# A two-layer diffusion transformer on one core: the feed-forward's work written out turn by turn, with every engine taking only what others finished in turns before

## The chip, the cores and the metric

The kernel runs on 1 NeuronCore of one Trainium2 chip. The core has a matrix engine (PE, with weight loads listed apart as PEld), a vector engine (DVE), a scalar engine (ACT), a general engine (POOL) and a queue for transfers (SP). Each works through its own instructions in the order written and waits on semaphores for the others. The metric is the device time of one execution in microseconds (us).

## The reference

Two layers over 512 latent tokens and 256 context tokens of width 1024. Each layer mixes tokens by two kinds of attention, and then runs a SwiGLU feed-forward. Every layer's norms and residuals are modulated by vectors that come from a condition: six rows of 1024 per layer, once for the latents and once for the context.

```python
mod = silu_c @ w_mod[l] + b_mod[l]
mod_c = silu_cc @ w_mod[l] + b_mod[l]
sh1, sc1, g1, sh2, sc2, g2 = jnp.split(mod[:, None, :], 6, axis=-1)
...
x = x + g1 * branch_merge(ya, yb, ga, gb, w_pa[l], w_pb[l], w_o[l])
...
h2 = modulate(rms_norm(x, norm2[l]), sh2, sc2)
x = x + g2 * swiglu(h2, w_ffn_in[l], w_ffn_out[l])      # a, u = split(h @ w_in); (silu(a) * u) @ w_out
if not last:
    hc2 = modulate(rms_norm(ctx, norm2[l]), csh2, csc2)
    ctx = ctx + cg2 * swiglu(hc2, w_ffn_in[l], w_ffn_out[l])
```

The hidden width is 2816, that is 22 blocks of 128 channels. Layer 0 runs the feed-forward on 768 tokens (latents and context), layer 1 on the 512 latents alone.

## The kernel before, in words

All data is float32, and each product is made of three matmuls on halves: an operand is split into an upper part that the matmul keeps exactly and a lower part that holds the rest, and the kernel adds upper·upper, upper·lower and lower·upper. ACT makes an upper part by a copy into the matmul's type, DVE the lower part by a subtraction.

A hidden block `f` needs gate and up weights (two raw tiles `wr` of 128x1024), each in two halves of the contraction, against two halves of the tokens (`nh` is 384 tokens in layer 0, 256 in layer 1). This 2x2 product is made by `quad` with seven products in place of eight, in the way of Strassen and Winograd. The left operands are the quarters A11, A12, A22 and the sums S1 = A21+A22 (in a tile `ws` of its own), S3 = A11-A21, S2 = S1-A11, S4 = A12-S2, written over the raw weights. The right operands are quarters of the activations and their sums, made before. Each product is one **turn** of PE: 12 matmuls (4 blocks of the contraction, 3 halves each). The order of turns, with the last of a block put behind the first of the next, is

A11, A22 of the block before, A12, S1, S2, S4, S3.

Products add up in three PSUM banks, `qu`, `qc` and `qv`. Because a bank is used again by a later turn, ACT first copies it to a tile `tt` (line 1728): `qu` after A11 and after S2, `qv` after S1. The second use of `qv` is turn S4, two turns after S1. Then DVE adds bank and copy (line 2140), ACT takes the silu of the sum (2141), DVE adds and multiplies for the up half (2153, 2154, 2157). The finished block `ph` is split in halves for the second matrix: ACT 1864, DVE 1865. After every four blocks an output part runs over eight column blocks `j`: weights `wfo` are split (ACT 1877, DVE 1881), 12 matmuls of 512 columns into a bank `po` (and in layer 0 another 12 of 256), and DVE adds the gated bank to the residual `x` (1577).

Blocks 0 and 1 (layer 0) and 0 to 2 (layer 1) run in the plain way ahead of this; the other 20 and 19 blocks and four output parts are written by `paced`. It sets the order on PE, DVE and ACT by hand: for each turn it writes first the weight work that later turns need (`load`: the transfer; `hi`: ACT's upper part, line 1585, and in the same call the DVE sums of S1, S2 and S4, lines 2115 to 2123; `lo`: DVE's lower part, line 1589), then the turn's matmuls, then what the bank needs (`take`). Upper parts are written up to three turns ahead and lower parts up to two.

`paced` also works off the modulation vectors: an item is a transfer of 512 KB (`wmodT`) and a DVE multiply-and-sum over 1024 elements for each condition (lines 450 and 452), two for most items of layer 0 and one for the others. An item is written once a count of spare DVE time allows it, both sums at once. The first output part waits (`gated`) until the items of its gate are done. Raw weights, modulation weights and output weights share four buffers `wr`; upper and lower parts share three buffers `wh` and three `wl`. Transfers are issued by SP; their order follows from the order of the code.

Of the kernel before, what the change touches and what calls it, by code (L numbers as in the profile page):

```python
# [331 lines left out]
class Trunk:  # L332
# [112 lines left out]
    def mod_one(self, l, n, crow, junk, w=None):  # L445
        nc, d = self.nc, self.d
        if w is None:
            w = self.raw(d["wmodT"][l * 48 + n])
# [3 lines left out]
        nc.vector.tensor_tensor_reduce(  # L452
            w, w, crow[:, 0], 1.0, 0.0, ALU.mult, ALU.add, self.mod[l][:, 0, n : n + 1])
# [1252 lines left out]
    def quad(self, left, right, kn, nh, take):  # L1706
# [19 lines left out]
        def copy(bank, name):  # L1726
# [15 lines left out]
                 load=left.load if w == "A11" else None, hi=lambda w=w: left.upper(w), lo=lambda w=w: left.lower(w),  # L1742
                 later=take.done if w == "A22" else None)
# [5 lines left out]
    def paced(self, steps, near, beside, ready):  # L1749


        at = [0.0]
        for s in steps:
            at.append(at[-1] + s.cost)
        done = dict(load=0, hi=0, lo=0)
        todo = sum(c for c, *_ in beside)
        share = min(1.0, 1.15 * todo / sum(s.cost - s.busy for s in steps))
        free, wait, late = 0.0, None, deque()
        self.live = 0

        def go(stage, up):
            while done[stage] < up:
                n = done[stage]
                if stage == "hi":
                    go("load", n + 1)
                    go("lo", n - 1)
                elif stage == "lo":
                    go("hi", n + 1)
                done[stage] += 1
                run = getattr(steps[n], stage)  # L1770
                if run:
                    if stage == "load" and self.live + 2 > 4 and wait:
                        beside_now()
                    run()

        def beside_now():
            nonlocal wait, free
            cost, run, w = wait
            run(w)
            self.live -= 1  # L1780
            free -= cost
            wait = None

        def fetch(n):
            nonlocal wait
            cost, load, run = beside.pop(0)
            wait = cost, run, load()
            self.live += 1
            return at[n]

        since = 0.0
        for n, s in enumerate(steps):
            count = lambda ahead: next((i for i in range(n, len(steps)) if at[i] >= at[n] + ahead), len(steps))
            far = count(4 * near + LEAD)
            while done["load"] < far and (not steps[done["load"]].load or self.live <= 2):
                go("load", done["load"] + 1)
            go("lo", max(n + 1, count(3 * near - 0.1)))
            go("hi", max(n + 1, count(4 * near - 0.1)))
            free = min(free + (s.cost - s.busy) * (share if ready() else 1.0), BEHIND)
            while s.gated and not ready():  # L1800
                if not wait:
                    fetch(n)
                beside_now()
            if wait and at[n] - since >= LEAD and free >= 0.7 * wait[0]:
                beside_now()
            if beside and not wait and self.live <= 2:
                since = fetch(n)
# [6 lines left out]
        while late:  # L1814
            late.popleft()()
        while wait or beside:
            if not wait:
                fetch(n)
# [133 lines left out]
    def run(self):  # L1952
# [3 lines left out]
        with (  # L1956
# [23 lines left out]
            for l in range(DEPTH):  # L1980
# [7 lines left out]
                with (  # L1988
# [33 lines left out]
                    def two(of, n, cost, then=None):  # L2022
                        def run(w):
                            self.mod_one(of, n, *rows, w)
                            if then:
                                then()
                        return cost, lambda: self.raw(d["wmodT"][of * 48 + n]), run
# [59 lines left out]
class Step:  # L2087


    def __init__(self, cost, busy, mul, take, load=None, hi=None, lo=None, later=None, gated=False):  # L2090
        self.cost, self.busy, self.mul, self.take = cost, busy, mul, take
        self.load, self.hi, self.lo, self.later, self.gated = load, hi, lo, later, gated


class Quarters:
# [14 lines left out]
    def upper(self, key):  # L2110
# [183 lines left out]
```

## Time and profile before

| | |
|---|---|
| median of 3 runs | 2081.72 us (2074.14 to 2083.82) |
| the profiled execution | 2073.19 us, of which 2070.6 us span |
| PE, PEld busy | 1951.0 us (94%), 1797.1 us (87%) |
| DVE, ACT, POOL busy | 1496.1 us (72%), 942.2 us (46%), 220.3 us (11%) |
| mean granted clock of PE | 0.985 |

The turns written by `paced` run from 654.0 to 1133.1 us (layer 0) and from 1670.2 to 2025.7 us (layer 1). In the views a row `PE qv L1722 <- ACT tt L1728` means that PE's matmuls into bank `qv` at line 1722 had to wait for ACT's copy at line 1728. Windows give the busy time of PE, PEld, DVE, ACT and POOL with the number of instructions, then the granted clock as a share of full speed, then the transfers' share and rate. In the chain of waits each row is a start, a length and a piece of work.

### The profile page before, as it was taken

How to read it: one execution, taken by the hardware profiler on the slowest of the kernel's cores; microseconds unless marked ns; L12 is line 12 of the kernel's file. 1: busy time of each engine (PE TensorE's matmuls, PEld its weight loads, DVE VectorE, ACT ScalarE, POOL GpSimd, SP SyncE). 2: the span in 40 equal slices, each digit the busy share in tenths (PEclk: the TensorE clock that was granted, in tenths of full speed). 3: DMA queues.
4: the chain of work that ended last, by engine and by line, in shares of the span. 5: the costliest groups of instructions: out<-in, count | busy, mean ns of one | idle time of the engine just before them, and what ended most of it. 6: DMA issues, size and time to landing. Idle time of an engine off the chain costs nothing. (4 is left out here: it accounts for less than half of the span.)

```text
span 2070.6 us, 31681 instructions
## 1 busy us (share of the span) xinstructions
PE 1951.0 (94%) x12298; PEld 1797.1 (87%) x12298; DVE 1496.1 (72%) x2813; ACT 942.2 (46%) x1832; POOL 220.3 (11%) x130
## 2 busy tenths in 40 slices
PE   8999999999999898989999999999999989889888
PEld 8989999888999888989888888799888988778777
DVE  7478887797778876776765777887566776666665
ACT  5466666622345323232423546665533453343344
POOL 0422232123000000000000031223100000000000
PEclk9999999999999999999999999999999999999999
DMA  8111112343631332434442421112245313213213
GB/s 308 51 57 47 49 62 70 103 172 133 224 118 41 107 127 83 131 97 148 131 134 74 148 92 37 41 57 75 95 157 211 105 57 97 82 60 104 82 60 121
DMA packets 73110, 214.79 MB, mean 104 GB/s; under 512 B 8704, under 2 KB 10880, under 8 KB 72960
## 3 DMA queue, kind: packets, MB, share of 16 engines
q1 hardware_dynamic: 72960, 212.78, 31.1%
q8 instruction: 96, 1.57, 0.3%
q14 instruction: 54, 0.44, 0.1%
HBM read 200.69 MB, written 6.82 MB: 100 GB/s over the span
## 5 line engine op out<-in xcount | busy, mean ns | idle before, releaser
L1722 PE MATMUL qu<-r,w 128*128 128x384 f32 (+1 forms) x1872 | 304.7, 316 | 8.7 <-ACT tt L1728 5.2
L1722 PEld LDWEIGHTS qu<-r,w 128*128 128x128 f32 x1872 | 288.5, 195 | 17.5 <-ACT tt L1728 7.6
L381 PE MATMUL pj<-h,wh 128*128 128x512 f32 (+1 forms) x704 | 256.8, 365 | 5.6 <-ACT kg L809 1.7
L381 PE MATMUL pj<-h,wl 128*128 128x512 f32 (+1 forms) x704 | 247.2, 351 | 0.0
L381 PE MATMUL pj<-hl,wh 128*128 128x512 f32 (+1 forms) x704 | 246.7, 350 | 0.0
L366 ACT ACTIVATE wh<-wr 128x1024 fp32r<-128x1024 f32 (+2 forms) x157 | 146.0, 936 | 210.0 <-issue 64.0
L1722 PE MATMUL qv<-r,w 128*128 128x384 f32 (+1 forms) x936 | 168.0, 333 | 71.7 <-ACT tt L1728 71.7
L1722 PEld LDWEIGHTS qv<-r,w 128*128 128x128 f32 x936 | 152.5, 207 | 80.9 <-ACT tt L1728 80.8
L1585 ACT ACTIVATE w<-wr 128x512 fp32r<-128x512 f32 x234 | 145.2, 624 | 166.7 <-DVE wr L2119 72.2
L381 PE MATMUL po<-ph,wh 128*128 128x512 f32 (+1 forms) x576 | 197.5, 344 | 1.6 <-ACT ph L1864 0.9
L381 PE MATMUL po<-ph,wl 128*128 128x512 f32 (+1 forms) x576 | 196.1, 342 | 1.5 <-DVE wl L368 1.4
L381 PE MATMUL po<-pl,wh 128*128 128x512 f32 (+1 forms) x576 | 195.8, 340 | 0.0
L1589 DVE TENSOR_TENSOR w<-wr,w 128x512 fp32r<-128x512 f32 x234 | 160.3, 687 | 46.3 <-ACT w L1585 44.1
L368 POOL TENSOR_TENSOR wl<-wr,wh 128x1024 fp32r<-128x1024 f32 (+1 forms) x66 | 145.3, 2205 | 389.9 <-ACT wh L366 383.6
L1577 DVE SCALAR_TENSOR_TENSOR x<-po,G,x 128x256 f32<-128x256 f32 (+3 forms) x168 | 99.3, 596 | 113.5 <-PE po L381 112.0
L381 PEld LDWEIGHTS pj<-h,wh 128*128 128x128 f32 x704 | 133.6, 190 | 20.4 <-ACT kg L809 1.9
L381 PEld LDWEIGHTS pj<-h,wl 128*128 128x128 f32 x704 | 133.2, 189 | 18.1
L381 PEld LDWEIGHTS pj<-hl,wh 128*128 128x128 f32 x704 | 133.8, 190 | 13.7
L505 POOL TENSOR_TENSOR rs<-rs,expo 128x2 f32<-128x2 f32 (+2 forms) x8 | 6.2, 773 | 1224.1 <-DVE rs L504 1224.1
L1009 ACT ACTIVATE pth<-tp 128x512 fp32r<-128x512 f32 x176 | 103.4, 596 | 64.6 <-PE tp L1059 37.1
L1010 DVE TENSOR_TENSOR ptl<-tp,pth 128x512 fp32r<-128x512 f32 x176 | 119.5, 685 | 15.2 <-ACT pth L1009 13.5
L381 PEld LDWEIGHTS po<-ph,wh 128*128 128x128 f32 x576 | 108.4, 188 | 15.9 <-ACT wh L366 2.2
(250 smaller groups left out, 4319.6 us busy)
## 6 DMA issues: line engine op xcount, KB each, us to landing
wr<-wfi SPq DMA_DIRECT2D x88, 512.0 KB, 3.3
wr<-wmodT SPq DMA_DIRECT2D x84, 512.0 KB, 3.3
wr<-win SPq DMA_DIRECT2D x68, 512.0 KB, 3.3
wr<-wfo SPq DMA_DIRECT2D x64, 256.0 KB, 2.7
wr<-wo SPq DMA_DIRECT2D x26, 512.0 KB, 3.6
wr<-wfo SPq DMA_DIRECT2D x26, 384.0 KB, 3.6
wr<-wp SPq DMA_DIRECT2D x32, 256.0 KB, 2.8
x<-x SPq DMA_DIRECT2D x16, 384.0 KB, 6.7
```

What stands on the lines that cost most here:

```text
L366: nc.scalar.activation(hi, raw, AF.Copy)
L368: (eng or nc.gpsimd).tensor_tensor(lo, raw, hi[:].bitcast(F32), op=ALU.subtract)
L381: nc.tensor.matmul(ps[:, : b - a], u[:, c], v[k][:, a:b], start=(k == 0 and i == 0), stop=(k == nk - 1 and i == 2),)
L505: nc.gpsimd.tensor_tensor(r[:, :nb], r[:, :nb], self.expo[:, :nb], op=ALU.pow)
L1009: nc.scalar.activation(hi, tp, AF.Copy)
L1010: nc.vector.tensor_tensor(lo, tp, hi[:].bitcast(F32), op=ALU.subtract)
L1577: self.nc.vector.scalar_tensor_tensor(x[j][:, f:u], ps[:, f - a : u - a], self.G[l][i][:, s, j : j + 1], x[j][:, f:u], op0=ALU.mult, op1=A ...
L1585: self.nc.scalar.activation(t[:, :n], src, AF.Copy)
L1589: self.nc.vector.tensor_tensor(t[:, n : 2 * n], src, t[:, :n].bitcast(F32), op=ALU.subtract)
L1722: nc.tensor.matmul(banks[bank], u[:, c], v, start=(first and k == 0 and i == 0), stop=(k == kn - 1 and i == 2), skip_group_check=True)
```

## The change

The diff leaves all arithmetic as it was and writes it in another order:

- The sums S1 to S4 get a stage of their own, `sum`, between `load` and `hi`. In front of a turn's matmuls `paced` now writes lower parts for three turns ahead, upper parts for four, and sums for five.
- `take` gives back work to be written one or two turns later: the silu, the product with the up half and the upper part of a finished block one turn later, the lower part of a finished block two turns later. It is written behind the lower parts and ahead of the upper parts and sums.
- The two sums of a modulation item are written one by one, each with half of the item's cost, and one is written as soon as half of its cost is spare; the count of spare time is a little faster (1.2 for 1.15).

```diff
-        if l == 0 or n < 16:
-            nc.vector.tensor_tensor_reduce(
-                junk, w, crow[:, 1], 1.0, 0.0, ALU.mult, ALU.add, self.mod[l][:, 1, n : n + 1])
-        nc.vector.tensor_tensor_reduce(
-            w, w, crow[:, 0], 1.0, 0.0, ALU.mult, ALU.add, self.mod[l][:, 0, n : n + 1])
+    def mod_parts(self, l, n, crow, junk):
...
+        return [part(s) for s in ((1, 0) if l == 0 or n < 16 else (0,))]
...
         def go(stage, up):
             while done[stage] < up:
                 n = done[stage]
-                if stage == "hi":
-                    go("load", n + 1)
-                    go("lo", n - 1)
-                elif stage == "lo":
-                    go("hi", n + 1)
+                if stage == "sum":
+                    go("lo", n - 2)
+                if stage != "load":
+                    go(order[order.index(stage) - 1], n + 1)
...
-            far = count(4 * near + LEAD)
+            ahead = lambda t: max(n + 1, next((i for i in range(n, len(steps)) if at[i] >= at[n] + t), len(steps)))
+            first, late, later = late, later, []
+            go("lo", ahead(3 * near + 0.1))
+            for run in first:
+                run()
+            go("hi", ahead(4 * near + 0.1))
+            go("sum", ahead(5 * near + 0.1))
+            far = ahead(5 * near + LEAD)
             while done["load"] < far and (not steps[done["load"]].load or self.live <= 2):
                 go("load", done["load"] + 1)
-            go("lo", max(n + 1, count(3 * near - 0.1)))
-            go("hi", max(n + 1, count(4 * near - 0.1)))
...
-            if wait and at[n] - since >= LEAD and free >= 0.7 * wait[0]:
+            if wait and at[n] - since >= LEAD and free >= 0.5 * wait[0][0]:
                 beside_now()
...
             s.mul()
-            while late:
-                late.popleft()()
-            s.take()
-            if s.later:
-                late.extend(s.later())
+            for delay, run in s.take() or ():
+                (late if delay == 1 else later).append(run)
...
     def silu(self, part, ps, more):
         nc = self.t.nc
         nc.vector.tensor_tensor(more, ps, more, op=ALU.add)
-        nc.scalar.activation(part, more, AF.Silu)
+        return [(1, lambda: nc.scalar.activation(part, more, AF.Silu))]
...
     def c22(self, ps, v1):
         v = self.t.nc.vector
         v.tensor_tensor(v1, ps, v1, op=ALU.add)
-        v.tensor_tensor(self.up, self.up, v1, op=ALU.mult)
+        return [(1, lambda: v.tensor_tensor(self.up, self.up, v1, op=ALU.mult))]
...
-    def done(self):
-        return self.parts(self.f)
+        return [*enumerate(self.parts(self.f), 1)]
```

The order on PE is the same but for a few matmuls at the two ends of the stage; POOL's is the same; DVE and ACT are written anew in the two stages, and SP's transfers of modulation, feed-forward and output weights change places among themselves in layer 0.

**DVE, layer 1**, one block, from the last product with `qu` of the block before to the sum of bank `qv`. Before (line 2118 and 2119 make S3 and S2, 2123 S4; 1589 lower parts; 2140 sums of banks `qc`, `qv` with their copies):

```order
L1589 TENSOR_TENSOR w_17949<-ws_17947,w_17949 128x512
L2118 TENSOR_TENSOR wr_17809<-wr_17807,wr_17809 128x512
L2119 TENSOR_TENSOR wr_17807<-ws_17947,wr_17807 128x512
L2157 TENSOR_TENSOR ph_17870<-ph_17870,qu_17816 128x256
L1589 TENSOR_TENSOR w_17969<-wr_17807,w_17969 128x512
L2123 TENSOR_TENSOR wr_17807<-wr_17807 128x512
L1865 TENSOR_TENSOR pl_17985<-ph_17870,ph_17984 128x512
L2140 TENSOR_TENSOR tt_17964<-qc_17990,tt_17964 128x256
L1589 TENSOR_TENSOR w_17988<-wr_17807,w_17988 128x512
L1589 TENSOR_TENSOR w_18009<-wr_17809,w_18009 128x512
```

After the change, the same block (2169 is the line that was 2157, 2152 was 2140, 1593 was 1589, 1870 was 1865):

```order
L2129 TENSOR_TENSOR wr_17800<-ws_17914,wr_17800 128x512
L2165 TENSOR_TENSOR tt_17892<-qu_17822,tt_17892 128x256
L1593 TENSOR_TENSOR w_17931<-ws_17914,w_17931 128x512
L2166 TENSOR_TENSOR ph_17872<-ph_17872,tt_17892 128x256
L2133 TENSOR_TENSOR wr_17800<-wr_17800 128x512
L1593 TENSOR_TENSOR w_17954<-wr_17800,w_17954 128x512
L2169 TENSOR_TENSOR ph_17872<-ph_17872,qu_17822 128x256
L1593 TENSOR_TENSOR w_17973<-wr_17800,w_17973 128x512
L2152 TENSOR_TENSOR tt_17970<-qc_17994,tt_17970 128x256
L1593 TENSOR_TENSOR w_17992<-wr_17802,w_17992 128x512
L1870 TENSOR_TENSOR pl_17989<-ph_17872,ph_17988 128x512
```

Every sum now stands two turns earlier (S3 and S2 ahead of the sum of bank `qu` two turns before, S4 ahead of the product with `qu` and no longer behind it), a turn's lower part comes first, and `pl` has moved from ahead of the `qc` sum to behind it.

**ACT, layer 1**, the same block, from the upper part of S1 to the copy of `qv`. Before:

```order
L1585 ACTIVATE w_17949<-ws_17947 128x512
L1728 ACTIVATE tt_17964<-qu_17951 128x256
L1585 ACTIVATE w_17969<-wr_17807 128x512
L1585 ACTIVATE w_17988<-wr_17807 128x512
L1864 ACTIVATE ph_17984<-ph_17870 128x512
L2141 ACTIVATE ph_18005<-tt_17964 128x256
L1585 ACTIVATE w_18009<-wr_17809 128x512
L1728 ACTIVATE tt_18024<-qv_18011 128x256
```

After:

```order
L1589 ACTIVATE w_17931<-ws_17914 128x512
L1589 ACTIVATE w_17954<-wr_17800 128x512
L1732 ACTIVATE tt_17970<-qu_17957 128x256
L1589 ACTIVATE w_17973<-wr_17800 128x512
L1869 ACTIVATE ph_17988<-ph_17872 128x512
L1589 ACTIVATE w_17992<-wr_17802 128x512
L2153 ACTIVATE ph_18007<-tt_17970 128x256
L1589 ACTIVATE w_18012<-wr_17935 128x512
L1732 ACTIVATE tt_18027<-qv_18014 128x256
```

Between two copies of banks there now stands one upper part per turn, each of a sum written on DVE a turn or more before.

**DVE, layer 0**, two sums of one modulation item (`ISA junk,mod` and `ISA wr,mod`, each followed by a read of its sum). Before:

```order
L2123 TENSOR_TENSOR wr_7454<-wr_7454 128x512
L450 ISA junk_5111,mod_105<-wr_7497,crow_5110 128x1024
L450 ISA mod_105 128x1
L452 ISA wr_7497,mod_105<-wr_7497,crow_5110 128x1024
L452 ISA mod_105 128x1
L1865 TENSOR_TENSOR pl_7552<-ph_7433,ph_7551 128x768
L2140 TENSOR_TENSOR tt_7531<-qc_7561,tt_7531 128x384
```

After:

```order
L1593 TENSOR_TENSOR w_7378<-wr_7264,w_7378 128x512
L449 ISA junk_5111,mod_105<-wr_7342,crow_5110 128x1024
L449 ISA mod_105 128x1
L2169 TENSOR_TENSOR ph_7299<-ph_7299,qu_7268 128x384
L1593 TENSOR_TENSOR w_7397<-wr_7264,w_7397 128x512
L449 ISA wr_7342,mod_105<-wr_7342,crow_5110 128x1024
L449 ISA mod_105 128x1
L2152 TENSOR_TENSOR tt_7394<-qc_7424,tt_7394 128x384
```

The two sums now stand in two turns, with a product and a lower part between them.

More of the change, by code (lines that the diff above doesn't have):

```diff
@@ L1754, in paced @@
             at.append(at[-1] + s.cost)
[L1755 to L1758, printed above, removed]
+        order = "load", "sum", "hi", "lo"
+        done = dict.fromkeys(order, 0)
+        share = min(1.0, 1.2 * sum(c for c, *_ in beside) / sum(s.cost - s.busy for s in steps))
+        free, wait, since = 0.0, [], 0.0
+        late, later = [], []
         self.live = 0
@@ L2116, in upper @@
         elif key == "S2":
+            assert "A11" in self.halves
             at["S3"], at["S2"] = at["A21"], at["A11"]
```

79 lines of the change are left out of this document (43 added, 36 removed).

## The prediction, made before the changed kernel was run

> **What bounds the kernel now.** I read the page first, for which engine fills the span, then who PE waits for, then the two stages that the diff touches, then the chain of waits inside one block.
>
> ```profile
> span 2070.6 us, 31681 instructions
> PE 1951.0 (94%) x12298; PEld 1797.1 (87%) x12298; DVE 1496.1 (72%) x2813; ACT 942.2 (46%) x1832; POOL 220.3 (11%) x130
> ```
>
> PE is busy for all but 119.6 us. The list of PE's waits says where most of that is (total, times, longest):
>
> ```profile
> PE qv L1722 <- ACT tt L1728: 71.7, 35, 3.0
> PE qu L1722 <- ACT tt L1728: 5.2, 5, 1.4
> PE qu L1722 <- DVE w L1589: 3.1, 14, 0.2
> ```
>
> 80.0 us, nearly all of one kind: turn S4 adds into bank `qv`, and must wait until ACT has copied what S1 left there. The windows of the two stages, in layer 0 and layer 1 (length, then busy time of PE, PEld, DVE, ACT, POOL, then the granted clock):
>
> ```profile
> 654.00:1133.06 479.06, 443.13 (x2473) 416.88 (x2472) 347.44 (x582) 159.41 (x291) 0.00 (x0) 0.99 0.35 113
> 1670.17:2025.72 355.55, 311.09 (x2012) 285.11 (x2011) 226.35 (x384) 137.22 (x279) 0.00 (x0) 0.94 0.26 81
> ```
>
> DVE and ACT are far from full in both, so the copy is late because of what it queues behind. The chain of waits in one block of layer 1 (start, length, work):
>
> ```profile
> 1757.59 0.61 DVE ws L2115
> ...
> 1760.28 0.70 DVE wr L2119
> ...
> 1761.07 0.64 ACT w L1585
> ...
> 1762.34 0.70 DVE wr L2123
> ...
> 1763.12 0.63 ACT w L1585
> 1763.75 0.53 ACT ph L1864
> ...
> 1764.30 0.69 DVE pl L1865
> 1764.99 0.35 DVE tt L2140
> ...
> 1765.68 0.61 ACT w L1585
> 1766.30 0.28 ACT tt L1728
> ...
> 1766.62 2.93 PE qv L1722 x12
> ```
>
> The work goes from DVE to ACT and back three times between the sum S1 (2115) and the copy (1728), and PE stands until it is through. That ring, not any engine's load, sets the time. The last row shows a second cost: 12 matmuls took 2.93 us, twice what they take where PE has not stood (1.44 below).
>
> How long would the stages take without the ring? The turns at full speed, from chains, the counts, and the output parts (the fourth row is PE's busy time in all `po` matmuls of one part of layer 0, which has no gap in it):
>
> ```profile
> 1673.05 1.44 PE qv L1722 x12
> 1784.99 2.79 PE po L381 x12
> 1789.22 19.56 PE po L381 x84
> 715.00:762.00 47.00, 33.99 (x192) 29.48 (x192) 9.84 (x16) 1.00 0.42 133
> 2020.67 3.60 PE po L381 x30
> 1123.80 2.08 PE qu L1722 x12
> 1125.88 5.10 PE po L381 x22
> L1722 PE MATMUL qv<-r,w 128*128 128x384 f32 x480 | 95.5, 348 | 30.4 <-ACT tt L1728 30.4
> L1722 PE MATMUL qv<-r,w 128*128 128x256 f32 x456 | 72.5, 316 | 41.3 <-ACT tt L1728 41.3
> ```
>
> Bank `qv` gets 24 matmuls a block, so there are 20 blocks in layer 0 and 19 in layer 1. Layer 0: 20 x 7 turns x 2.08 + 4 parts x 33.99 + 5.10 = 432.3 of the window's 479.1 us, so 46.8 lost. Layer 1: 19 x 7 x 1.44 + 4 x (2.79 + 19.56) + 3.60 = 284.5 of 355.6, so 71.1 lost. Together 117.9 us can be won: the 80.0 us of waits and some 38 us of matmuls at a low clock.
>
> **The change, part by part.** No arithmetic is added or removed, so the floor of the two stages is that of the sums above. What counts is whether the new order leaves a wait.
>
> *Sums two turns, upper and lower parts one turn earlier; bank work one or two turns later.* I lay out DVE's work in layer 1 by PE's turns, with 0.61 us for 512 columns and 0.35 for 256 (from start to next start in the rows 2115 and 2140 above). Each turn has one lower part. Beside it stand: A11, a product and S4 (1.57 in all); A22, a product (0.96); A12, the `qc` sum (0.96); S1, `pl` (1.22); S2, nothing (0.61); S4, the sum S1 and the `qv` sum (1.57); S3, two sums and the `qu` sum (2.18). In all 9.07 us for 7 x 1.44 = 10.08 of PE. The worst stretch begins with the `qv` sum, which ends 0.35 after PE's turn S4; the work of S3 then ends 2.53 after that turn, 1.09 behind PE's S3; A11's ends 1.22 behind, A22's 0.74, A12's 0.35, and by S2 DVE is ahead again. Who needs it then? A lower part is needed three turns on. The `qu` sum must be read before turn A22 writes the bank, 1.44 after S3's end: 0.35 us of room, the smallest. ACT's copy of `qv` in turn S1 now stands behind one silu and one upper part, which can start 0.35 after A12's end and take 0.42 and 0.61 or so; the copy is then on time at S1's end, and done a turn before S4 needs it. The ring is cut: the upper parts of S1, S2, S4 wait for sums of a turn before, and `pl` stands behind the `qc` sum, a turn after ACT made its operand.
>
> The measured rows agree that this is close but fits (busy times as above; the first two are whole blocks from stall to stall, the third seven output columns):
>
> ```profile
> 1750.51:1766.62 16.11, 13.19 (x84) 12.78 (x85) 9.69 (x18) 6.14 (x14) 0.00 (x0) 0.82 0.21 66
> 1004.53:1020.72 16.19, 14.87 (x86) 14.55 (x85) 12.85 (x22) 7.01 (x13) 0.00 (x0) 1.00 0.36 124
> 1789.22:1808.78 19.56, 19.56 (x86) 15.80 (x86) 10.42 (x16) 4.42 (x8) 0.00 (x0) 1.00 0.40 135
> ```
>
> A block of layer 1 holds 9.69 us of DVE for 10.08 of PE, one of layer 0, two modulation sums included, 12.85 for 14.56, and an output part about half.
>
> *Modulation sums one by one.* A sum costs what it did:
>
> ```profile
> L452 DVE CUSTOM_DVE_ANT_0 wr<-wr,crow 128x1024 f32<-128x1024 f32 x46 | 56.2, 1221 | 0.8
> L1589 DVE TENSOR_TENSOR w<-wr,w 128x512 fp32r<-128x512 f32 x112 | 76.7, 688 | 18.8 <-ACT w L1585 16.7
> L2154 DVE TENSOR_TENSOR ph<-ph,tt 128x256 f32<-128x256 f32 x19 | 8.1, 425 | 2.0
> ```
>
> Both at once hold DVE for 2.4 us, more than a turn of 2.08; one holds it for 1.2, and in the new order they stand in turns A22 and A12, which have little else. This saves nothing of its own; it keeps the bound above true in layer 0. One burst stays: ahead of the first output column of layer 0 four sums still stand in a row, some 5 us, with the residual behind them; PE has two output columns and a turn A22 to run before it needs a weight from behind them, 2 x 33.99 / 8 + 2.08 = 10.6 us.
>
> *What the new order may cost.* The trace has no row for a wait that does not exist yet, so I bound it per block. Below: nothing, since no dependency in the layout is overrun. Above: DVE by its full row lengths, 12 x 0.69 + 5 x 0.425 = 10.4 us in layer 1, 0.3 over PE's, and up to 0.7 for the hand-overs at its four bank sums, so 1.0 us; the same in layer 0, where the room is larger. I take 0.25 in layer 1 (the room of 0.35 is the smallest, so it is nearest to the row lengths) and 0.15 in layer 0. For each of the eight output parts 0 to 1.5 us, and I take 0.5.
>
> *Transfers.* SP issues the same transfers, in layer 0 in another order among themselves; POOL's queue is untouched and idle here. Weights are now asked for about a turn earlier, but lower parts free their buffers a turn earlier too. Landing and the waits for it in layer 0:
>
> ```profile
> DMA to landing us min/median/max: 3.1/3.3/4.9
> ACT w L1585 <- DMA wr<-wfi: 15.5, 10, 2.7
> ```
>
> A block's first buffer is free at turn A22 or A12 and its weights are wanted at S1 or later; two turns and the copy's spare turn cover the median landing. I take nothing for it; its price if the cover goes is the last rival.
>
> **Sum.** 2073.2 (the profiled execution, 2070.6 of it span) - 117.9 + 19 x 0.25 + 20 x 0.15 + 8 x 0.5 = **1967 us**. The median of the runs shown, 2081.72, lies 8.5 above the profiled execution. The waits are what could vary between runs, and they go, so I stay at the profiled base; with the offset it would be 1976.
>
> The Trainium skill, in "TensorE: Matmul & The Clock Gate" (Part 1, on the clock gate), says that PE's clock is halved only after an idle window of about 3.4 us. The longest wait here is 3.0 us, so by that rule the slow matmuls have another cause and would stay. The trace speaks against it: the clock was 0.82 in the window of a block with such a wait, and 1.00 in the output part without one.
>
> **Rivals.**
> - *DVE becomes the bound.* For it: 9.69 of 10.08 us. Against it: output parts let it catch up, and the busy time counts the overlapping ends of instructions. At 1.0 us per block and 1.5 per output part, 2073.2 - 117.9 + 39 + 12 = 2006 us.
> - *The low clock stays.* Only the 80.0 us of waits go, the slow matmuls remain: 2073.2 - 80.0 + 11.8 = 2005 us. Against it: the two clocks just named. This is where the skill's rule would lead.
> - *The ring is only shortened.* The copy of `qv` still stands behind a silu that waits for DVE. If half of the loss remains: 2073.2 - 59 = 2014 us. Against it: the layout has a whole turn of room there.
> - *A slower kernel: late weights.* DVE's sum S1 (2115 before) reads a raw tile two turns sooner. If that tile lands late, all that DVE has queued behind the sum, bank sums and lower parts, is late with it, and ACT's silus and copies after them. To cost more than the 106 us won, 39 blocks must each lose a wait X beyond DVE's room, 19 (X - 0.4) + 20 (X - 1.7) > 106, so X > 3.8 us. At the longest landing, 4.9, the kernel would take 2073.2 - 106 + 19 x 4.5 + 20 x 3.2 = 2117 us. For it: ten waits for weights are there now. Against it: they add up to 15.5 us, and transfers fill a third of the engines' time.
>
> **Chances.** The forecast (1955 to 1985) 0.68; DVE's bound 0.15; the clock 0.06; the shortened ring 0.06; slower 0.04; no real change 0.01. The bounds of the unknown costs give 2073.2 - 117.9 = 1955 and 2006; with the neighbouring cases the range is 1955 to 2010. A difference under 0.5% of 2081.72, some 10 us, I count as no change. Faster 0.94, same 0.02, slower 0.04.
>
> **What would show it.** In the new profile the row of `qv` waiting for the copy should fall from 71.7 us to under 10, the clock in the layer 1 stage should rise from 0.94 to 0.99 or more, and the stages should take about 440 and 292 us. ACT's waits for the sums may stay; they cost nothing. If PE waits in turn A22 for DVE's `qu` sum, DVE is the bound. If PE's waits are gone but its turns still take 2.9 us, the clock has another cause. If DVE waits for `wfi` at the sum S1, the weights are late, and the prediction fails.

## The result, and the profile after

The changed kernel takes 1964.97 us (median of 4, 1961.76 to 1967.77), the kernel before 2078.22 us in the same rounds (2074.14 to 2083.82). The ratio is 0.9453 (95% interval 0.942 to 0.9486). The prediction was 1967 us, in a range of 1955 to 2010. The ratios leave out one execution, of the version with only the sums split, that took 3811.28 us where its other nine took 2068 to 2077.

The head of the page of the changed kernel, and its chain that ended last by engine:

```profile
span 1965.1 us, 31571 instructions
PE 1920.8 (98%) x12298; PEld 1777.7 (90%) x12298; DVE 1479.8 (75%) x2813; ACT 948.9 (48%) x1832; POOL 220.1 (11%) x130
...
PE 66%; DVE 6%; issue 3%; ACT 2%; DMA 0%; POOL 0%; DVEq 0%; POOLq 0%; ACTq 0%
```

PE is idle for 44.3 us in place of 119.6, and has done the same matmuls in 30.2 us less of busy time. DVE and ACT have the busy times of before within 17 us. The list of PE's waits (total, times, longest; the lines of the file have moved by a few, so 1722 is now 1726, and 1728 is 1732):

```profile
PE qu L1726 <- ACT tt L1732: 1.9, 4, 0.5
PE qv L1726 <- ACT tt L1732: 1.7, 5, 0.3
```

The wait for the copy of `qv` fell from 71.7 to 1.7 us. The windows of the two stages, and one of layer 1 without a passage to or from an output part in it (columns as in the prediction):

```profile
655.00:1088.67 433.67, 433.14 (x2478) 414.12 (x2477) 338.06 (x582) 163.54 (x291) 0.00 (x0) 1.00 0.39 125
1626.70:1920.37 293.67, 290.09 (x2013) 268.58 (x2012) 219.88 (x384) 140.23 (x279) 0.00 (x0) 1.00 0.31 98
1696.00:1734.00 38.00, 38.00 (x270) 35.51 (x269) 27.62 (x50) 18.69 (x39) 0.00 (x0) 1.00 0.29 85
```

Layer 0 went from 479.06 to 433.67 us, 1.4 above its floor of 432.3; layer 1 from 355.55 to 293.67, 9.2 above its floor of 284.5. Together that is 107.3 us, and the profiled execution (1967.19 us) is 106.0 us shorter than the one of before. The granted clock is 1.00 in both. In the third row PE is busy for all 38.00 us and DVE for 27.62, 73%. That row can hide short delays of PE: the record of a matmul of 256 columns is 0.28 us long, and the next one starts 0.12 us after it.

One group of ACT keeps a large idle time (busy and mean ns of one, then the idle time before it and what ended most of it):

```profile
L1589 ACT ACTIVATE w<-wr 128x512 fp32r<-128x512 f32 x234 | 145.4, 625 | 103.5 <-DVE wr L2129 39.3
```

The upper parts still wait for DVE's sums. Inside the blocks they now wait ahead of need, so PE does not.

Most of what is left in layer 1 stands where an output part ends and a block begins. The timeline there (start, length, work; in brackets the idle time before it and what ended it):

```profile
1681.76 0.74 DVE L1581 SCALAR_TENSOR_TENSOR x<-po,G,x 128x512 f32<-128x512 f32 x1
...
1683.62 0.69 DVE L2133 TENSOR_TENSOR wr<-wr 128x512 f32<-128x512 f32 x1
1684.43 0.63 ACT L1589 ACTIVATE w<-wr 128x512 fp32r<-128x512 f32 x1 [1.86 <-DVE wr L2133]
1684.96 0.37 ACT L1732 ACTIVATE tt<-qu 128x256 f32<-128x256 f32 x1
...
1685.38 1.70 PE L1726 MATMUL qu<-r,w 128*128 128x256 f32 x12 [0.48 <-ACT tt L1732]
...
1687.41 1.69 PE L1726 MATMUL qv<-r,w 128*128 128x256 f32 x12 [0.34 <-ACT tt L1732]
```

DVE's residual of the last output column (1581) and two lower parts stand ahead of the sum S4 (2133); the sum is late, the upper part of S4 on ACT waits 1.86 us for it, and the copy of `qu` stands behind that upper part. Each of the four passages loses 1.3 us of PE, measured from start to start of its matmuls. The rest is a short delay in most blocks, shown below with DVE.

### The profile page after: what moved, and what is told of

Its sections match the earlier page's. It is cut to its first block, busy times and chain, and to the rows that moved or that the text cites. A ratio compares the mean times of both kernels' runs of the same rounds, so it can differ in the third digit from the quotient of the medians.

```text
span 1965.1 us, 31571 instructions
## 1 busy us (share of the span) xinstructions
PE 1920.8 (98%) x12298; PEld 1777.7 (90%) x12298; DVE 1479.8 (75%) x2813; ACT 948.9 (48%) x1832; POOL 220.1 (11%) x130
## 4 chain that ended last, share of the span: by engine, by line
PE 66%; DVE 6%; issue 3%; ACT 2%; DMA 0%; POOL 0%; DVEq 0%; POOLq 0%; ACTq 0%
PE po L381 19%; PE qu L1726 13%; PE pj L381 10%; PE qv L1726 7%; PE pp L381 4%; PE qc L1726 3%; PE pf L381 3%; PE pv L954 1%; PE sc L1037 1%; PE y L1073 1%; PE tp L1063 1%; PE sc L1164 1%; PE y L1200 1%; DVE w L1593 1%; PE tp L1188 1%
## 5 line engine op out<-in xcount | busy, mean ns | idle before, releaser
L1726 PE MATMUL qu<-r,w 128*128 128x384 f32 (+1 forms) x1872 | 295.4, 310 | 1.9 <-ACT tt L1732 1.9
L1726 PEld LDWEIGHTS qu<-r,w 128*128 128x128 f32 x1872 | 281.1, 189 | 6.5 <-ACT tt L1732 2.7
L1589 ACT ACTIVATE w<-wr 128x512 fp32r<-128x512 f32 x234 | 145.4, 625 | 103.5 <-DVE wr L2129 39.3
L1726 PE MATMUL qv<-r,w 128*128 128x384 f32 (+1 forms) x936 | 151.1, 310 | 1.7 <-ACT tt L1732 1.7
L1726 PEld LDWEIGHTS qv<-r,w 128*128 128x128 f32 x936 | 141.1, 190 | 2.8 <-ACT tt L1732 2.7
```

Source lines behind the costliest of these rows:

```text
L1589: self.nc.scalar.activation(t[:, :n], src, AF.Copy)
L1726: nc.tensor.matmul(banks[bank], u[:, c], v, start=(first and k == 0 and i == 0), stop=(k == kn - 1 and i == 2), skip_group_check=True)
```

## The experiments

The theory is that of the prediction: before the change a ring sum on DVE, upper part on ACT, bank sum on DVE, copy on ACT closed inside a block, and the fixed order cuts it. Three questions were open: which of the edits cuts the ring, how near DVE is to being the bound, and whether the low clock comes from the stands. "Before" below is the kernel before in the same rounds, and times are medians.

### Which part of the change does it?

**The modulation sums alone.** The kernel before, with this one edit of the change:

```diff
-        share = min(1.0, 1.15 * todo / sum(s.cost - s.busy for s in steps))
+        share = min(1.0, 1.2 * todo / sum(s.cost - s.busy for s in steps))
...
-            wait = cost, run, load()
+            w = load()
+            wait.extend((cost / len(some), lambda f=f: f(w)) for f in some)
...
-            if wait and at[n] - since >= LEAD and free >= 0.7 * wait[0]:
+            if wait and at[n] - since >= LEAD and free >= 0.5 * wait[0][0]:
```

> The kernel before, with the modulation sums written one by one (each with half the cost, the count of spare time a little faster, as in the change), and the order of the feed-forward work left as it was. My theory: the ring between DVE and ACT sets the loss, and it is there without any modulation sum (layer 1 has none in this stage). Layer 1's stage stays at 355 us, layer 0's falls from 479 to 465 or so because a burst of 1.2 us in place of 2.4 lies in the ring: 2064 us (2050 to 2078). Rival, the bursts are what makes layer 0's copies late: its stage falls to 440 us, 2035 us in all.

2073.25 us against 2078.26, ratio 0.9976 (0.9961 to 0.999). Its waits:

```profile
PE qv L1726 <- ACT tt L1732: 66.7, 36, 2.7
PE qu L1726 <- ACT tt L1732: 7.2, 8, 1.4
```

Splitting the sums, with the slightly faster count that is part of the edit, is worth some 5 us (2 to 8 by the interval). The prediction gave it no gain of its own, and the expectation gave it 14; the ring is untouched.

**Taking back the order part by part.** Three kernels, each the changed one with an edit taken back: the sums written only when an upper part needs them (no turn ahead of it); the bank work written where it stood before (silu and product at once, the halves of a finished block behind the next turn's matmuls); and both.

```diff
-            go("sum", ahead(5 * near + 0.1))
```
```diff
-            for delay, run in s.take() or ():
-                (late if delay == 1 else later).append(run)
...
+            for run in held:
+                run()
+            held = [run for _, run in s.take() or ()]
...
-        return [(1, lambda: nc.scalar.activation(part, more, AF.Silu))]
+        nc.scalar.activation(part, more, AF.Silu)
...
-        return [(1, lambda: v.tensor_tensor(self.up, self.up, v1, op=ALU.mult))]
+        v.tensor_tensor(self.up, self.up, v1, op=ALU.mult)
...
-        return [*enumerate(self.parts(self.f), 1)]
+        return [(0, run) for run in self.parts(self.f)]
```

> The changed kernel, but S1 to S4 are written again together with their upper parts (four turns ahead, in the same turn), not a turn before; bank work stays one and two turns late. My theory: the upper part then waits for DVE within its turn, about 3.2 us after the end of S3 for S2, 5.8 for S4, and through the qc sum the copy of qv ends some 8.1 us after it, where turn S4 could start at 7.2: 0.9 us lost per block of layer 1, 0.3 in layer 0, so 1965 + 23 = 1988 us (1972 to 2002). Rival, the sums alone make the ring: most of the loss returns, over 2040 us. Other rival, the sums' place is of no account: 1965 us.

> The changed kernel, but silu and product are written at once after the bank sum, and the halves of a finished block behind the next turn's matmuls, as before; the sums stay a turn ahead of their upper parts. My theory: pl stands again ahead of the qc sum and waits for ACT; that sum ends 1.6 us after turn A12 in place of 0.35, and the copy of qv some 0.2 to 0.3 us too late in layer 1, not late in layer 0: 1965 + 5 = 1970 us (1964 to 1982). Rival, the late bank work is what cuts the ring: over 2040 us.

> The changed kernel with both of the last two edits together: sums with their upper parts, and bank work at once; the upper and lower parts stay a turn earlier than before and the modulation sums one by one. My theory: the two delays stand in one ring and add up on top of its room, so the loss is far more than the sum of the two alone: the copy of qv ends 2.2 us too late in layer 1, with half-speed matmuls behind it, and 1.6 us in layer 0: 1965 + 42 + 27 + 32 = 2066 us (2035 to 2080). Rival, the two edits act apart: the sum of their losses alone, about 1993 us. Other rival, the turn more of lead for upper and lower parts is what won the time: 1965 to 1975 us.

Sums late: 1993.42 us, ratio 0.9594 (0.9565 to 0.9624). Bank work at once: 1967.29, ratio 0.9472 (0.9447 to 0.9496). Both: 2027.74, ratio 0.9766 (0.9737 to 0.9795). So the late bank work buys nothing that can be measured as long as the sums come a turn ahead, and 34 us once they don't. The first two times lie in their expected ranges. The two edits are not additive: 28 and 2 us apart, 63 together. That speaks for a ring, which is cut at either place. The first and the third kernel's waits:

```profile
PE qv L1726 <- ACT tt L1732: 20.8, 22, 1.4
```
```profile
PE qv L1726 <- ACT tt L1732: 40.7, 33, 2.1
```

But with both taken back the kernel is still 45 us faster than the one with the split sums alone, and my expectation (2066) missed that by 38. What those two still differ in is mainly the turn by which upper and lower parts stand further ahead of their matmuls.

**The extra turn.** The kernel with the bank work at once, and lower parts, upper parts and sums each one turn nearer to their use; a sum is still written a turn ahead of the upper part that reads it.

```diff
-            go("lo", ahead(3 * near + 0.1))
+            go("lo", ahead(2 * near + 0.1))
...
-            go("hi", ahead(4 * near + 0.1))
-            go("sum", ahead(5 * near + 0.1))
-            far = ahead(5 * near + LEAD)
+            go("hi", ahead(3 * near + 0.1))
+            go("sum", ahead(4 * near + 0.1))
+            far = ahead(4 * near + LEAD)
```

> The changed kernel with the bank work at once (which was worth nothing alone, 1967 us), and with the upper and lower parts and the sums each a turn nearer to their use: upper and lower parts stand as far ahead as before the change, but the sums are still made a turn before the upper parts that read them. Theory: it is the order sum, then upper, then lower, each a turn apart, that opens the ring, and the extra turn of distance to the matmuls is worth little with it: 1970 us (1965 to 1985). Rival: the extra turn is worth by itself what two other runs differ by (2073 us without both, 2028 us with the extra turn alone, 45 us): 2010 us or more.

1981.11 us against 2079.30, ratio 0.9532 (0.9516 to 0.9548). Its stages:

```profile
657.99:1098.00 440.01, 434.06 (x2472) 414.27 (x2472) 341.17 (x582) 162.60 (x291) 0.00 (x0) 0.99 0.39 123
1634.62:1936.08 301.46, 290.87 (x2012) 268.61 (x2010) 222.47 (x384) 138.02 (x279) 0.00 (x0) 1.00 0.31 96
```

With the bank work at once, four kernels now stand beside each other:

| | upper and lower parts as far ahead as before | one turn further |
|---|---|---|
| sums written with the upper part | 2073.25 | 2027.74 |
| sums written a turn ahead of it | 1981.11 | 1967.29 |

(The first of them is the kernel before with split sums, whose rules of order differ in details too.) Sums a turn ahead alone win 92 of the 106 us (less or more by what those details are worth, which no run shows), the extra turn alone 45, the late bank work nothing on top. The ring was cut mainly on DVE's side.

### How near is DVE to being the bound?

DVE's lower part of A11 made three times, then five times, in every block, so two and four operations more; nothing else changes.

```diff
-        self.halves[key] = self.t.lower(self.halves.pop(key + "+"), self.at[key], self.n)
+        up = self.halves.pop(key + "+")
+        for _ in range(3 if key == "A11" else 1):
+            self.halves[key] = self.t.lower(up, self.at[key], self.n)
```

> The changed kernel with DVE's lower part of A11 made three times over in each block (two more operations of 128x512, with the same result), to see how far DVE is from being the bound. Two accounts of DVE's load in a block of layer 1: by start to next start 9.07 us of PE's 10.08, by busy time 9.69. Two more are 1.22 us. My theory, start to start counts: 10.29 us, 0.2 over PE in layer 1 and nothing in layer 0, 1965 + 4 = 1969 us (1964 to 1976). Rival, busy time counts: 10.91 us, 0.8 over, 1965 + 16 = 1981 us (1977 to 1990).

> The same with four more operations, 2.44 us a block. My theory, start to start: 11.51 us in layer 1, 1.4 over PE's 10.08, and 15.1 us against 14.56 in layer 0's blocks with two modulation sums: 1965 + 27 + 8 = 2000 us (1988 to 2015), DVE then without idle time in layer 1's blocks. Rival, busy time: 2.05 us over in layer 1 and 0.7 in layer 0, 1965 + 54 = 2019 us.

Two more: 1989.81 us, ratio 0.9571 (0.9545 to 0.9597). Four more: 2053.22, ratio 0.9875 (0.984 to 0.9911). Both accounts expected less. The timeline of layer 1 with two more:

```profile
1709.82 0.42 DVE L2167 TENSOR_TENSOR tt<-qu,tt 128x256 f32<-128x256 f32 x1
...
1710.30 1.69 PE L1726 MATMUL qu<-r,w 128*128 128x256 f32 x12 [0.50 <-DVE tt L2167]
...
1715.14 2.74 DVE L1593 TENSOR_TENSOR w<-wr,w 128x512 fp32r<-128x512 f32 x4
...
1721.13 1.10 PE L1726 MATMUL qu<-r,w 128*128 128x256 f32 x7 [0.51 <-DVE tt L2167]
```

PE stands once in a block, in turn A22, for DVE's sum of bank `qu`. That is the place which the prediction named as the one with the smallest room. A block now takes 1721.13 - 1710.30 = 10.83 us. The four lower parts hold DVE for 2.66 us up to its next start, and two held it for 1.32 in the changed kernel, so the two more cost 1.34 us and not 1.22.

The changed kernel itself has no room left at that turn:

```profile
1691.95 1.49 PEld L1726 LDWEIGHTS qu<-r,w 128*128 128x128 f32 x12 [0.17 <-DVE tt L2165]
...
1701.79 0.42 DVE L2165 TENSOR_TENSOR tt<-qu,tt 128x256 f32<-128x256 f32 x1
...
1702.26 1.49 PEld L1726 LDWEIGHTS qu<-r,w 128*128 128x128 f32 x12 [0.18 <-DVE tt L2165]
...
1709.83 0.42 DVE L2152 TENSOR_TENSOR tt<-qv,tt 128x256 f32<-128x256 f32 x1 [0.72 <-PE qv L1726]
```

The sum ends at 1702.21, and the first weight load of A22 waits for it. By the starts of the matmuls before it the turn was due at 1702.13, so the sum is 0.08 us late, where the prediction had it 0.35 us early. With 0.10 us more behind the turn's first matmul, a block takes 1702.26 - 1691.95 = 10.31 us in place of 10.08. So the two more operations lengthen a block by 0.52 us, and the other 0.82 of their 1.34 went into time in which DVE had waited, for bank `qv` above all (0.72 us in the last row).

DVE's own load is what my account said: in that block of the changed kernel the starts of its operations add up to 9.04 us when the waits are taken out (estimated from the trace), against 9.07. What the account left out is the order. DVE waits for the bank of turn S4, and then has two sums and a lower part to do before the `qu` sum that PE needs. So PE can wait for DVE in every block while DVE is idle 0.72 us in the same block.

With four more, the two stages were (columns as in the windows above):

```profile
655.00:1119.00 464.00, 442.55 (x2480) 416.85 (x2478) 392.83 (x663) 160.57 (x292) 0.00 (x0) 0.99 0.36 117
1654.00:2005.00 351.00, 309.16 (x2014) 285.48 (x2012) 269.74 (x460) 141.20 (x280) 0.00 (x0) 0.95 0.26 82
```

They are 30 and 57 us longer than in the changed kernel. In layer 1 the granted clock fell to 0.95 and PE was busy 19 us longer for the same matmuls, a cost that neither account had.

### Does the low clock come from the stands?

ACT's copy of `qv` in the changed kernel made 8 times, and 12 times, in every block. Nothing but PE's turn S4 needs it soon.

```diff
-            nc.scalar.activation(kept[name], banks[bank], AF.Copy)
+            for _ in range(8 if name == "v1" else 1):
+                nc.scalar.activation(kept[name], banks[bank], AF.Copy)
```

> The changed kernel with ACT's copy of qv after S1 made eight times over (seven more, 0.28 us each in layer 1 and about 0.39 in layer 0), so that turn S4 has to wait in each block: 2.0 and 2.7 us later, less about 1.0 and 1.6 us of room, some 1.0 us of standing in both layers. It asks what a short stand costs. My theory, as the waits of 1.5 us before cost: no low clock (0.99 or more in both stages), 1965 + 19 x 1.0 + 20 x 1.1 = 2006 us (1990 to 2020). Rival, any stand lowers the clock: layer 1's clock under 0.96 and 2020 us or more.

> The same with eleven more copies: some 2.1 us of standing per block in layer 1 and 2.7 us in layer 0, all under 3.4 us. My theory, stands of 2 to 3 us halve the clock for a turn or so behind them: layer 1's clock under 0.95, layer 0's under 0.99, 1965 + 19 x 2.1 + 20 x 2.7 + 20 for the slow matmuls = 2079 us (2060 to 2100). Rival (the Trainium skill, TensorE: Matmul & The Clock Gate, Part 1, an idle window of about 3.4 us before the clock falls): the clock stays at 0.99 or more and only the stands cost, 2059 us or less.

With 8 copies: 2082.76 us, ratio 1.0018 (1.0003 to 1.0034). With 12: 2189.52, ratio 1.0531 (1.0494 to 1.0568). Both were missed by far, by some 77 and 110 us. The reason is first in the copies. Timeline of the kernel with 8, in layer 0 and then in layer 1:

```profile
800.61 2.24 PE L1726 MATMUL qu<-r,w 128*128 128x384 f32 x12
800.80 4.16 ACT L1733 ACTIVATE tt<-qv 128x384 f32<-128x384 f32 x8 [0.20 <-PE qv L1726]
...
805.01 2.36 PE L1726 MATMUL qv<-r,w 128*128 128x384 f32 x12 [2.16 <-ACT tt L1733]
...
1751.58 0.61 ACT L1589 ACTIVATE w<-wr 128x512 fp32r<-128x512 f32 x1
...
1752.10 3.28 ACT L1733 ACTIVATE tt<-qv 128x256 f32<-128x256 f32 x8
...
1755.43 2.60 PE L1726 MATMUL qv<-r,w 128*128 128x256 f32 x12 [3.25 <-ACT tt L1733]
...
1765.65 1.60 PE L1726 MATMUL qu<-r,w 128*128 128x256 f32 x12
1769.20 2.70 PE L1726 MATMUL qv<-r,w 128*128 128x256 f32 x12 [1.95 <-ACT tt L1733]
```

A copy in such a row costs 0.52 us in layer 0 (4.16 / 8) and 0.41 in layer 1. The 0.28 in the chain of before is the time to ACT's next start; the copy itself lasted 0.36 there. In the second stand an upper part stood ahead of the copies on ACT, in the third nothing did. The room is one turn less one copy and the 0.20 us until it starts: in the changed kernel the copy of `qv` ended 0.85 us ahead of turn S4.

Then the clock. Twelve matmuls take 1.60 us in layer 1 and 2.24 in layer 0 where PE has not stood. After a stand of 1.95 us in layer 1 they took 2.70, after 3.25 us 2.60; after 2.16 us in layer 0 only 2.36. With 12 copies, layer 0:

```profile
803.21 3.76 PE L1726 MATMUL qv<-r,w 128*128 128x384 f32 x12 [4.24 <-ACT tt L1733]
```

The stages of the two kernels (8 copies, then 12):

```profile
656.00:1143.00 487.00, 444.01 (x2476) 419.01 (x2475) 338.85 (x582) 230.19 (x431) 0.00 (x0) 0.99 0.35 111
1680.00:2039.00 359.00, 314.20 (x2017) 291.40 (x2016) 219.79 (x384) 190.88 (x412) 0.00 (x0) 0.93 0.25 80
```
```profile
653.00:1203.00 550.00, 466.61 (x2481) 441.25 (x2479) 338.98 (x583) 269.41 (x512) 0.00 (x0) 0.94 0.31 98
1741.00:2142.00 401.00, 324.75 (x2010) 302.22 (x2009) 220.17 (x384) 219.78 (x488) 0.00 (x0) 0.89 0.23 72
```

In layer 0 the clock was 1.00 without stands, 0.99 with stands of about 2.2 us, 0.94 with stands of 4.24 (the median of 20). If all were like the one shown, 20 blocks x (4.24 of stand + 3.76 - 2.24 of slow matmuls) = 115 us, and the stage is 116 us longer than in the changed kernel. So the low clock follows the stands, in a kernel where nothing but ACT's copies changed. ACT's copies are not the cause by themselves: with four more operations on DVE, PE stood for DVE, ACT made no copy more, and layer 1's clock was 0.95.

The stands with 12 copies came out at 4.24 us in layer 0 and at 3.6 (median) in layer 1, so over the 3.4 us of the expectation: that run cannot part the two accounts. The kernel with 8 copies does. In layer 1 its stands of 1.95 and 3.25 us were followed by slow matmuls and a clock of 0.93, as the rival of that expectation had it and my theory had not; in layer 0, with 2.16 us, the clock stayed at 0.99. What makes the difference is in the last section.

### Does a sum one turn sooner take the last waits?

> The changed kernel itself, for a comparison in the same rounds: 1965 us (1962 to 1968).

1964.35 us against 2079.30, ratio 0.945 (0.9434 to 0.9467): the base for the next kernel, whose edit is

```diff
-            go("sum", ahead(5 * near + 0.1))
-            far = ahead(5 * near + LEAD)
+            go("sum", ahead(6 * near + 0.1))
+            far = ahead(6 * near + LEAD)
```

> The changed kernel with its modulation sums made six turns ahead in place of five, and the loads two such turns more. What is left of the waits in the L1 stage stands at the four passages from an output part to the next block, about 0.64 and 0.49 us each, since the upper part of S4 waits on ScalarE for a sum that VectorE makes only behind its residual step. Theory: with the sum made a turn sooner the upper part isn't late, the eight waits go, 4 x 1.1 = 4.5 us: 1960.5 us (1958 to 1964). Rival: the residual step of VectorE is then late for something else (the output banks, the lower part of S4), and the time stays: 1963 to 1967.

By the edit the loads stand one turn further ahead than in the changed kernel, not two.

1974.96 us against 2079.30, ratio 0.9506 (0.9489 to 0.9522), so 10.6 us slower than the changed kernel. Its layer 1 stage and what PE and SP did behind layer 0:

```profile
1639.26:1927.00 287.74, 285.95 (x2011) 267.50 (x2010) 218.12 (x384) 138.97 (x279) 0.00 (x0) 1.00 0.32 100
```
```profile
PE po L381 <- ACT wh L366: 13.3, 1, 13.3
```
```profile
1070.26 20.39 SPq L357 DMA_DIRECT2D wr<-wmodT  x8
1091.46 8.53 SPq L357 DMA_DIRECT2D wr<-wfo  x6
```

The theory held in the main where it was aimed: layer 1 became 5.7 us shorter (it took 293.42 us in the changed kernel of the same rounds). The waits for ACT's copies at the passages went; PE now waits there in turn A22 for DVE's `qu` sum, 0.5 us where passage and turn lost 1.6 before, so four passages gain 4.2 us. Another 2.1 us come from the nine other blocks, which the expectation had not counted: S3 and S2 now stand ahead of the `qv` sum, in the time that DVE had waited, and the 0.23 us of turn A22 are gone there. The loss is elsewhere. The sooner loads hold raw buffers longer, the modulation items beside the stage are written later for want of them, and seven of their sums ran on DVE only after layer 0's last turn. Eight transfers of modulation weights then went ahead of the output weights on SP's queue, and PE stood 13.34 us for the first of these. It is a form of the prediction's late-weights rival, in another place.

**The same, with the loads nearer.** The sums six turns ahead, the loads a turn nearer than in the changed kernel, by which no item is left over:

```diff
-            go("sum", ahead(5 * near + 0.1))
-            far = ahead(5 * near + LEAD)
+            go("sum", ahead(6 * near + 0.1))
+            far = ahead(4 * near + LEAD)
```

> The changed kernel with its modulation sums made six turns ahead in place of five, as in the version at 1975 us, and the weight loads a turn later, so that the two stages hold as many raw weights as in the changed kernel and the pieces of modulation weights that go beside the first stage are used up before it ends (seven of them were left over in that version, and TensorE then stood 13.34 us for the output weights loaded behind theirs). Theory: the L1 stage keeps that version's gain (293.4 to 287.7 us) and the wait behind the L0 stage goes: 1959 us (1957 to 1963). Rival: the sums now wait for the loads, which stand only two turns ahead of the first sum (3.2 us from issue to landing against 2 x 1.4 us plus LEAD's rest in L1), VectorE stands behind them, and the gain is gone: 1964 us or more.

1958.73 us (1955.49 to 1961.75), ratio 0.9447 (0.9427 to 0.9467) to its before, 2076.03. The stages:

```profile
653.38:1085.41 432.03, 431.98 (x2473) 413.08 (x2472) 342.55 (x582) 159.99 (x291) 0.00 (x0) 1.00 0.39 125
1620.52:1908.26 287.74, 285.94 (x2012) 267.47 (x2010) 218.30 (x384) 138.89 (x279) 0.00 (x0) 1.00 0.32 100
```

The wait behind layer 0 is gone and layer 1 keeps its 287.74 us. It came as expected, and by the stages it is the fastest kernel here. For the whole time the two measures disagree: its five executions all lie below the eight of the changed kernel (1961.76 to 1967.77), but it was not run in the same rounds, and by the ratios, 0.9447 and 0.945, the two cannot be told apart.

## Why the prediction was right, point by point

- **The loss and the floor.** 117.9 us above the floor, of which 11.75 was to stay. Left are 1.4 us in layer 0 and 9.2 in layer 1, 10.6 together. 2073.2 - 117.9 + 10.6 = 1965.9, and the profiled execution took 1967.19.
- **How the residual is made up** was right in one piece and wrong in the others. It was 4.75 us for blocks of layer 1, 3.0 for those of layer 0, 4.0 for output parts. From start to start of the matmuls, 14 blocks of layer 1 lose 0.23 us each in turn A22, 3.3 in all: the place that was named, and nearly the 0.25 that was taken. The four passages from an output part to a block lose 1.3 each, 5.4 in all, and the entry into the first block 0.7; 0.5 a part was taken, within 0 to 1.5. All of layer 0 loses 0.9 (1.4 by the length of its stage), where 3.0 and four times 0.5 were taken. One term was too small and one too large, so that the total came within 2 us is in part luck.
- **The ring.** The wait for the copy of `qv` was to fall below 10 us and fell to 1.7; the stages were to take about 440 and 292 us and take 434 and 294. ACT's waits for sums stayed in part: 107.8 us in the list of waits (39.3, 34.7 and 33.8), against 259.0 before (132.0, 72.2 and 54.8). That they cost nothing was right inside the blocks, and wrong at the four passages.
- **Bank work one or two turns later.** The prediction put both moves into one term. The runs part them: the sums and the extra turn give the 106 us, the late bank work gave nothing measurable beside them.
- **DVE's room.** The walk through the turns found the right place (turn A22, the `qu` sum) and 0.35 us of room, where the sum is 0.08 late. Three steps were too short: the `qv` sum starts 0.27 us after its turn's end and not at once, S2 starts 0.72 after S3 and not 0.61, and PE waits for the whole 0.42 of the `qu` sum and not 0.35. The load itself, 9.07 us a block, was right. The prediction's sign "if PE waits in turn A22 for DVE's `qu` sum, DVE is the bound" is too simple: PE waits there although DVE is idle in the same block, and the kernel with sums a turn sooner removes that wait in nine of the fourteen blocks with the same work on DVE. Two operations more in a block brought the wait to 0.75 us over PE's 10.08.
- **The clock.** Its rise to 1.00 was forecast, and the runs with repeated copies show the cause: stands bring it down. The rival that the slow matmuls would stay, to which the Trainium skill's rule led ("TensorE: Matmul & The Clock Gate", Part 1, an idle window of about 3.4 us), is refuted as applied to the length of single stands: 1.95 us was enough here.
- **Late weights.** Not in this kernel; but one turn more on the loads brought a form of it, with 13.3 us.
- **The median** of before was to be left aside for the profiled execution, which gave 1967 us in place of 1976. In the same rounds before had 2078.22 us, so the gain is 113 us by medians, and 106 by the profiled executions.

## What to carry to other kernels

When three engines hand work around in a ring and none is full, look for the work that one engine queues ahead of what another waits for, and write each piece a turn ahead of its reader; one such cut gave 92 of 106 us here, a turn more of distance most of the rest, and a second cut at another place of the same ring nothing more. A list of busy times does not show the last of it: an engine can be waited for while it is idle elsewhere in the same block, so look at the starts. Count the matmuls that run slowly after a stand as part of the price of the stand. Moving work earlier takes buffers earlier: count what else lives in them, since here one turn more on the loads turned a gain of 6 us into a loss of 11.

## What the runs showed of the hardware beyond what was expected

- **Stands well under 3 us can cost a slow stretch behind them, and the length of the stand alone does not decide it.** Twelve matmuls took 2.70 for 1.60 us after a stand of 1.95 us in layer 1, but 2.36 for 2.24 after 2.16 us in layer 0. The clock records of the traces show why. In all 14 traces the clock drops from 1.00 to 0.50, every drop that ends within the trace lasts 3.41 us or a whole number of times that, and the drops of a trace lie on one fixed grid of 3.413 us. Cut by that grid, the kernel with 8 copies around these two stands (layer 0, then layer 1):

```profile
800.12:803.53 3.41, 2.73 (x16) 2.41 (x14) 1.47 (x3) 3.06 (x7) 0.00 (x0) 1.00 0.58 203
803.53:806.94 3.41, 1.93 (x11) 1.93 (x12) 1.29 (x2) 2.79 (x6) 0.00 (x0) 1.00 0.00 0
806.94:810.36 3.42, 3.42 (x22) 3.42 (x21) 2.85 (x6) 1.35 (x3) 0.00 (x0) 1.00 0.27 79
...
1766.09:1769.50 3.41, 1.46 (x12) 1.25 (x11) 0.55 (x1) 3.19 (x9) 0.00 (x0) 1.00 0.19 78
1769.50:1772.92 3.42, 3.42 (x18) 3.42 (x17) 2.20 (x4) 1.41 (x5) 0.00 (x0) 0.50 0.44 139
1772.92:1776.33 3.41, 3.41 (x31) 3.41 (x30) 3.38 (x8) 1.57 (x4) 0.00 (x0) 1.00 0.05 19
```

  The first stand is split between two windows, which keep PE busy for 2.73 and 1.93 us, and the clock stays. The second lies almost whole in one window, PE is busy for 1.46 us of it (43%), and the next window runs at half the clock. Over all full-speed windows of the 14 traces, those with PE busy for under 45% were followed by a slow one in 105 of 107 cases, those with 45 to 55% in 31 of 90, and those with more in 4 of 7876. So a stand costs its own length, and where it leaves a window less than about half busy, some 1.5 to 1.7 us more. The Trainium skill ("TensorE: Matmul & The Clock Gate", Part 1) describes a free-running window of about 3.4 us and half the clock behind an idle one; a window at half the clock would cost 1.7 us, an estimate from that page. The traces agree on the window and on the cost, but a window that was 43% busy counted as idle here.
- **An operation that must wait for the one just before it on its own engine starts later than one that need not.** DVE's lower part of A11, repeated on one tile, started 0.72 us after the one before, and the next one, of the same form on another tile, 0.61. S2, which writes a tile that S3 reads, started 0.72 after S3. ACT's copy of 256 columns started 0.42 us after the one before in a row of eight, each of which waits for ACT's own semaphore, and ACT's next operation 0.28 after the last of them.
